# Hybrid decoder layer: seven block products instead of eight in both MLP matmuls, left factors kept in DRAM, MLP moved around the second attention

## The chip, the cores and the metric

The kernel runs on one core of a Trainium2 chip. The metric is the device time of one launch in microseconds. Inputs, weights and output are float32 in DRAM; one launch computes one decoder layer for 2048 tokens of width 1024.

## What is computed

The reference, cut to the parts that the change touches (the mixer, attention on dilated windows beside a gated linear recurrence, stays as it is):

```python
def reference(x, ...):
    h = rms_norm(x, mix_norm_pre)
    m = hybrid_mixer(h, w_in, ..., w_out)          # 2048 x 1024
    x = x + rms_norm(m, mix_norm_post)
    h = rms_norm(x, mlp_norm_pre)
    return x + rms_norm(squared_relu_mlp(h, w_ff_in, w_ff_out), mlp_norm_post)

def squared_relu_mlp(h, w1, w2):                   # w1 1024 x 4096, w2 4096 x 1024
    a = jax.nn.relu(h @ w1)
    return (a * a) @ w2
```

## The kernel before

Every large product is made of float32 operands that are split into a leading part and the rest (`split`, L51: a copy with rounding on ACT, L53, and a subtraction, L54, on DVE or GpSimd). A product of two split operands takes three matmuls on TensorE (leading by leading, leading by rest, rest by leading), each of one 128x128 block against 512 columns.

The work comes in these stages.

- **Input projection and first attention.** The 1024 x 2560 product `z` (L197 to L199) for all tokens, in two halves of 1024 tokens, the recurrent branch on four channel tiles (`recurrent_block`), and the attention of the first half of the queries, four pairs of heads (`attention`, hf 0). The string ORDER names the sequence of these pieces. q, k, v and the mixer's output `mix` go to DRAM (`scr`).
- **Output projection** of a half, eight tiles of 128 tokens (`out_proj_tile`, `proj_norm`): 48 matmuls of 128x512 into `m` (L615 to L617), then on ACT the sum of squares (L624), on DVE the norm (L66 to L74), the product with the gain (L626), the sum with x (L627), on ACT again a sum of squares; the result x2 goes to DRAM (L628). `make_h2` multiplies by the second norm (L593) and turns the tile with eight transposes on TensorE (L599), and splits it: h2, the MLP's input.
- **Second attention** (hf 1), four pairs of heads.
- **MLP** (`mlp`) in three passes: tokens 0 to 511, 512 to 1023, and 1024 to 2047. Each pass goes over the 32 blocks of the inner axis of 4096: `z = h2 @ w1` (L884 to L886, 24 matmuls for 512 tokens), relu and square on ACT (L888, L889), then `o = a @ w2` (L767 to L769), added up in SBUF on DVE (L773, `y`). In the second product the passes two and three take Strassen's seven products of half blocks instead of eight for eleven and fourteen of the sixteen pairs of inner blocks; the sums of blocks of `w2` (L726, GpSimd) and of `a` (L726, DVE) are made for each pair. The first product is plain in all passes. w1 and w2 are loaded and split once for each pass.

What sets the order: a scheduler at build time orders each engine's instructions by a simulated timeline, within the dependencies and the buffers of the pools. So the first pass of the MLP runs amid the second attention, the second output projection (OPT, H2T: at which pair of inner blocks a tile is put in) amid the second pass, and the third pass by itself. SP issues nearly all loads and stores in one queue, in order; GpSimd issues the stores of `mix` and x2 and, at the end of the first two passes (`finish_all`), four accumulating loads of x2 into `y` (L813) and four stores of the result (L814), each store behind the landing of its load.

```python
for t in range(NT):
    tt = tt0 + t
    v.scalar_tensor_tensor(out=y[t], in0=y[t], scalar=r[:, t:t + 1], in1=g4t[0], ...)   # L812
    g.dma_start(out=y[t], in_=scr["x2"][tt], accum_op=ALU.add)                          # L813
    g.dma_start(out=out[tt // NC, tt % NC], in_=y[t])                                   # L814
```

Names in the profile: `z` with h2Ha, h2Hb or h2La is the MLP's first product, `z` with hH the input projection; `o` the MLP's second product with `B`, `A` (seven products) or `w2t`, `a` (plain); `S`, `SB`, `pT`, `oA`, `oB` are the attention's scores, turned probabilities and values; `kh`, `kl`, `vb` its loads; `mraw`, `mH`, `mL` the output projection's input, raw and split.

Of the kernel before, what the change touches and what calls it, by code (L numbers as in the profile page):

```python
# [40 lines left out]
def by_residue(ap):  # L41
    """512 tokens as they are stored, by (residue mod 4, quotient)."""
    return ap.rearrange("p (c m) -> p c m", c=NC)


def in_time(ap):
    """512 tokens in the order of time, seen by (residue, quotient)."""
    return ap.rearrange("p (m c) -> p c m", c=NC)


def split(nc, hi, lo, src, lo_eng=None):  # L51
    """src = hi + lo exactly; hi carries the leading bits, lo the rest."""
    nc.scalar.copy(out=hi, in_=src)  # L53
    (lo_eng or nc.vector).tensor_tensor(out=lo, in0=src, in1=f32(hi), op=ALU.subtract)  # L54


def rsqrt_mean(nc, pool, ss, k, name, eps, e=None):
    """1 / sqrt(ss / D + EPS) for ss [P, k]."""
# [27 lines left out]
class Project:  # L86
    """Input projection and recurrent branch, one half of the tokens at a time."""
# [25 lines left out]
    def load_start(self, ct, px):  # L113
        """the first weights and the first block of x^T, as the first product needs them."""
# [16 lines left out]
    def load_norm(self, tb, px=None):  # L131
        """1 / rms of a block of tokens, tokens on partitions."""
# [17 lines left out]
    def load_x(self, tb, px=None, also=None):  # L150
        """x^T times the gain, split; the norm's factor comes in after the products."""
# [4 lines left out]
        for k in range(KT):  # L156
            # x waits in the place that the next part of the lower halves takes
# [21 lines left out]
    def spread_norm(self, tb):  # L179
        """The norm's factors of a block along the free axis, on all partitions."""  # L180
# [21 lines left out]
    def qkv(self, hf, pr):  # L202
        """q, k, v of a pair of heads."""
# [42 lines left out]
    def recurrent_consts(self, conv_w, conv_b, w_r, b_r, w_i, b_i, lam):  # L246
# [14 lines left out]
        # hs = softplus(-lam); log1p(e) = 2 atanh(e / (2 + e))  # L261
# [20 lines left out]
        # the last inputs of the convolution and the last state, per channel tile  # L282
# [5 lines left out]
    def recurrent(self, hf, cs, w=None, px=None, pz=None):  # L288
        """the recurrent branch of some channel tiles."""
# [5 lines left out]
    def recurrent_block(self, hf, c, b, wx, wg, px, pz):  # L295
# [20 lines left out]
        # sigmoid(z) = (1 + tanh(z / 2)) / 2  # L316
# [3 lines left out]
        # a = exp(-L); 1 - a^2 = tanh(L) (1 + a^2)  # L320
# [14 lines left out]
        # gelu(x) = x / 2 * (1 + tanh(sqrt(2 / pi) * (x + 0.044715 x^3)))  # L335
# [15 lines left out]
def attention(tc, p, ps, cst, scr, hf, mask_a_d, mask_b_d, bufs):  # L351
# [27 lines left out]
    def across(t, i):  # L379
        """the last run of a block of 512 tokens and the first of the next, seen as runs() does."""  # L380
        a = t[:, (i - 1) * TB + 3 * MR:(i + 1) * TB]
        return bass.AP(a.tensor, a.offset, [list(a.ap[0]), [3 * P + MR, 2], [P, NC], [1, MR]])

    def probs(part, n):
        tags, bufs, n = (("thA", "tlA"), 1, n) if part == "A" else (("thB", "tlB"), 2 - hf, n)
# [8 lines left out]
    def softmax_rows(st, u, cols, sp, sm, parts, mask, name):  # L394
        """exp(S + mask - max) of the parts (columns, width) of one bank, with max and sum."""
# [14 lines left out]
    def pair(pr):  # L410
        st = {k: p.tile([P, 2, 2, NQH], F32, tag=f"st{k}", bufs=2, name=f"st{k}{hf}_{pr}") for k in "AB"}
        na = p.tile([P, HT], F32, tag="na", bufs=1, name=f"na{hf}_{pr}")
        nb = p.tile([P, HT], F32, tag="nb", bufs=1, name=f"nb{hf}_{pr}")
        va = p.tile([P, NQH + hf, 2 * P], F32R, tag="va", bufs=1, name=f"va{hf}_{pr}")
        for c in range(NC):
            cs = slice(c * MR, (c + 1) * MR)
            if hf:
                t0 = TB + c * P + P - MR
                nc.sync.dma_start(out=f32(va[cs, 0, :]), in_=f32(scr["v"][0][pr][t0:t0 + MR, :]))
            for i in range(NBH):  # L420
                t0 = i * TB + c * P
                nc.sync.dma_start(out=f32(va[cs, hf + 4 * i:hf + 4 * i + 4, :]),
                                  in_=f32(scr["v"][hf][pr][t0:t0 + P, :].rearrange("(n m) d -> m n d", m=MR)))
        for u in range(2):
            h = 2 * pr + u
            n_ = f"{hf}_{h}"
            row = slice(u * HD, (u + 1) * HD)
            ud = slice(u * P, (u + 1) * P)
            qs = p.tile([P, HT], F32R, tag="qs", bufs=bufs, name=f"qs{n_}")
            kh = p.tile([P, NK], F32R, tag="kh", bufs=bufs, name=f"kh{n_}")  # L430
            kl = p.tile([P, NK], F32R, tag="kl", bufs=bufs, name=f"kl{n_}")
            vb = p.tile([P, NX * NC, P], F32R, tag="vb", bufs=1, name=f"vb{n_}")
# [727 lines left out]
```

## Time and profile before

| | |
|---|---|
| median of 3 launches | 2399.44 us (2397.65 to 2401.24) |
| span of the profiled execution, first to last instruction | 2394.6 us |
| median less that span | 4.84 us |
| TensorE, matmuls | 10798, busy 2287.9 us (96%) |
| VectorE (DVE) / ScalarE (ACT) / GpSimd (POOL) busy | 1637.8 / 1158.5 / 1047.8 us |
| moved by DMA | 298.96 MB, mean 125 GB/s |

How to read it: the span is one execution; the launch time has some microseconds around it. A busy share of TensorE counts overlapped matmuls once; an idle time is what no matmul covers. PEclk is the share of the full TensorE clock that was granted. Stages by time from the span's start: to about 640 us input projection and first attention, to 745 us the first output projection, to 1275 us the second attention with the first MLP pass, to 1750 us the second pass with the second output projection, then the third pass.

### The profile page before, as it was taken

Reading aid. Unit: us, or ns where it says so; the run is one execution under the profiler, and the core shown is the slowest. Engines: PE = TensorE matmul, PEld = TensorE weight load, DVE = VectorE, ACT = ScalarE, POOL = GpSimd, SP = SyncE. Lnnn points to the kernel's source line nnn. Section 1 sums busy time; section 2 is a strip of 40 time slices with the busy share of each in tenths; the row PEclk is TensorE's granted clock in tenths of the full one; section 3 lists DMA queues with packets and bytes.
Section 4 is the critical chain, followed back from the end, with each engine's and each line's share of the span. In section 5 each row is a group of like instructions: output and inputs, shape, how many; then the busy total and the mean of one; then the engine's idle time right before and its main releaser. Section 6 shows DMA issues by size and latency. Waiting matters only on the chain. (4 is left out here: it accounts for less than half of the span.)

```text
span 2394.6 us, 31821 instructions
## 1 busy us (share of the span) xinstructions
PE 2287.9 (96%) x10798; PEld 1873.9 (78%) x10798; DVE 1637.8 (68%) x2991; ACT 1158.5 (48%) x2353; POOL 1047.8 (44%) x820
## 2 busy tenths in 40 slices
PE   8989999999998999999999989999989999999997
PEld 6668878677886888888887768887778888888886
DVE  6848577983353566666775998669647777677676
ACT  7537465663234555555564544445363333333332
POOL 5543324446221113131323667555365555555544
PEclk9999999999999999999999999999999999999999
DMA  8364775217647464546465333344411111111114
GB/s 278 102 163 131 200 214 142 67 62 227 182 137 202 110 170 126 163 136 167 123 160 162 119 119 106 116 154 159 127 53 58 49 53 53 53 54 49 53 58 137
DMA packets 183058, 298.96 MB, mean 125 GB/s; under 512 B 20224, under 2 KB 79008, under 8 KB 182896
## 3 DMA queue, kind: packets, MB, share of 16 engines
q1 hardware_dynamic: 175376, 271.40, 38.7%
q0 software_dynamic: 7520, 25.53, 3.3%
q8 instruction: 86, 1.41, 0.2%
q14 instruction: 76, 0.62, 0.1%
HBM read 246.39 MB, written 50.46 MB: 124 GB/s over the span
## 5 line engine op out<-in xcount | busy, mean ns | idle before, releaser
L773 DVE TENSOR_TENSOR y<-o,y 128x512 f32<-128x512 f32 x464 | 307.4, 681 | 125.0 <-PE o L769 124.6
L54 POOL TENSOR_TENSOR w2t<-w2r,w2t 128x512 fp32r<-128x512 f32 x92 | 138.6, 1521 | 427.0 <-ACT w2t L53 423.0
L884 PE MATMUL z<-h2Ha,w1H 128*128 128x512 f32 x768 | 304.8, 397 | 9.5 <-ACT sq L888 9.2
L885 PE MATMUL z<-h2La,w1H 128*128 128x512 f32 x768 | 302.4, 394 | 0.0
L886 PE MATMUL z<-h2Ha,w1L 128*128 128x512 f32 x768 | 302.3, 394 | 0.0
L197 PE MATMUL z<-hH,wH 128*128 128x512 f32 x640 | 261.5, 409 | 15.9 <-ACT wH L53 7.4
L198 PE MATMUL z<-hL,wH 128*128 128x512 f32 x640 | 260.8, 408 | 0.6 <-DVE hL L172 0.6
L199 PE MATMUL z<-hH,wL 128*128 128x512 f32 x640 | 260.3, 407 | 0.0
L54 POOL TENSOR_TENSOR B<-w2r,B 128x512 fp32r<-128x512 f32 x125 | 195.0, 1565 | 86.8 <-ACT B L53 86.3
L767 PE MATMUL o<-B,A 128*128 128x512 f32 x546 | 211.7, 394 | 12.0 <-DVE y L773 7.0
L768 PE MATMUL o<-B,A 128*128 128x512 f32 x546 | 214.1, 392 | 1.6 <-POOL B L54 1.6
L53 ACT CAST w1H<-w1r 128x512 fp32r<-128x512 f32 x192 | 112.2, 619 | 212.7 <-PE z L885 169.2
L769 PE MATMUL o<-B,A 128*128 128x512 f32 x546 | 213.5, 392 | 1.5 <-DVE A L54 1.5
L884 PEld LDWEIGHTS z<-h2Ha,w1H 128*128 128x128 f32 x768 | 145.5, 190 | 41.3 <-ACT sq L888 11.3
L886 PEld LDWEIGHTS z<-h2Ha,w1L 128*128 128x128 f32 x768 | 145.7, 190 | 30.0
L885 PEld LDWEIGHTS z<-h2La,w1H 128*128 128x128 f32 x768 | 146.0, 190 | 29.5
L197 PEld LDWEIGHTS z<-hH,wH 128*128 128x128 f32 x640 | 122.5, 191 | 48.6 <-ACT wH L53 8.0
L768 PE MATMUL o<-w2t,a 128*128 128x512 f32 x400 | 157.7, 397 | 1.7 <-POOL w2t L54 1.7
L767 PE MATMUL o<-w2t,a 128*128 128x512 f32 x400 | 157.3, 402 | 0.1
L769 PE MATMUL o<-w2t,a 128*128 128x512 f32 x400 | 156.0, 394 | 0.0
L54 POOL TENSOR_TENSOR wL<-wraw,wH 128x512 fp32r<-128x512 f32 x74 | 103.9, 1418 | 111.4 <-ACT wH L53 92.8
L198 PEld LDWEIGHTS z<-hL,wH 128*128 128x128 f32 x640 | 122.3, 191 | 31.4 <-issue 4.3
(271 smaller groups left out, 5620.5 us busy)
## 6 DMA issues: line engine op xcount, KB each, us to landing
w1r<-in_dram SPq DMA_DIRECT2D x192, 256.0 KB, 2.8
w2r<-in_dram SPq DMA_DIRECT2D x192, 256.0 KB, 2.9
wraw<-in_dram SPq DMA_DIRECT2D x79, 256.0 KB, 3.6
kh<-sk SPq DMA_DIRECT2D x48, 256.0 KB, 5.9
kl<-sk SPq DMA_DIRECT2D x48, 256.0 KB, 7.6
vb<-sv SPq DMA_DIRECT2D x24, 512.0 KB, 5.0
xr<-in_dram SPq DMA_DIRECT2D x32, 256.0 KB, 5.8
xn<-in_dram SPq DMA_DIRECT2D x16, 512.0 KB, 6.8
```

What stands on the lines that cost most here:

```text
L53: nc.scalar.copy(out=hi, in_=src)
L54: (lo_eng or nc.vector).tensor_tensor(out=lo, in0=src, in1=f32(hi), op=ALU.subtract)
L197: pe.matmul(z, hi[:, k, :], hh, start=(k == 0), stop=False)
L198: pe.matmul(z, hi[:, k, :], hl, start=False, stop=False)
L199: pe.matmul(z, lo[:, k, :], hh, start=False, stop=(k == KT - 1))
L767: pe.matmul(o, a[:, 0, ts], b[:, 0, :], start=(j == 0), stop=False)
L768: pe.matmul(o, a[:, 0, ts], b[:, 1, :], start=False, stop=False)
L769: pe.matmul(o, a[:, 1, ts], b[:, 0, :], start=False, stop=(j == len(pairs) - 1))
L773: v.tensor_tensor(out=dst, in0=o, in1=dst, op=ALU.add)
L884: pe.matmul(z, wh[:, k, :], hh[:, k, :], start=(k == 0), stop=False)
L885: pe.matmul(z, wh[:, k, :], hl[:, k, :], start=False, stop=False)
L886: pe.matmul(z, wl[:, k, :], hh[:, k, :], start=False, stop=(k == KT - 1))
```

## The change

Both MLP products are made as Winograd's form of Strassen's scheme with seven products throughout, and the MLP goes by halves of 1024 tokens instead of three passes.

- **MLP input** (`mlp_in`): for two blocks of the inner axis at a time (a pair, 16 in a half), tokens and model axis in halves. Seven products of 12 matmuls of 128x512 (L844 to L846) go into three banks zA, zB, zC; sums of w1 blocks are made on GpSimd, the four results are put together on ACT and DVE in `sq`. Two pairs run interleaved (TURNS). The right factors are sums of blocks of h2 (`Factors`), made tile by tile in the output projection (`columns`) and at its end (`finish`). Of each pair the seven left factors of the second product (`a`, 1792 KB) are stored to DRAM; in the first half also the sums of w2 (1024 KB a pair, from a load of 1024 KB) for both halves. w1 is read once for each half (1024 KB a pair).
- **MLP output** (`mlp_out`): the seven products one after the other, each over all 16 pairs: a factor pair of 256 KB + 256 KB is loaded (L948 and L954 or L956), split on ACT, DVE and GpSimd, and used for 12 matmuls (L964 to L966), four banks of 128x512 accumulating over the 16 pairs in PSUM. The rings of split factors have 3 places in the first half and 16 in the second.
- **Place:** first output projection, MLP input of the first half, then the second attention with the steps of the first half's MLP output put between its own by a written order (`interleave`, two steps of three matmuls at each place, TensorE's order by hand), the load of w_out, the second output projection, then the second half's MLP input and output. The last piece of the input projection (q13) comes after the first attention's pools are closed.
- **Attention:** loads of the second half's keys as one DMA for both copies, buffers for the next head's loads, and its own pieces cut so that the next scores stand before the present values. Nothing of what it computes changes.

```diff
-def mlp(tc, p, pc, pw, ps, cst, scr, T, tt0, h2T, w1, w2, g4, out, nb1, nb2, ...):
...
+LEFT = {1: "A11", 2: "A12", 3: "S4", 4: "A22", 5: "S1", 6: "S2", 7: "S3"}
+RIGHT = {1: "B11", 2: "B21", 3: "B22", 4: "T4", 5: "T1", 6: "T2", 7: "T3"}
...
+class Factors:
+    EARLY, LATE = ("B11", "B21", "B22"), ("T2", "T3", "T1", "T4")
...
+    def columns(self, p, ps, ident, tt, x2, rs2, g3b):
+        v.scalar_tensor_tensor(out=h2, in0=x2, scalar=rs2[:, tt:tt + 1], in1=g3b, op0=ALU.mult, op1=ALU.mult)
+        for q in range(2):
...
+                nc.tensor.transpose(pt[:, i * P:(i + 1) * P], h2[:, k * P:(k + 1) * P], ident)
+            (v.tensor_copy if q else nc.scalar.copy)(out=R[q][th][:, :, cs], in_=pt.rearrange("p (k t) -> p k t", t=P))
+        if th == 0:
+            self.split("B11", b11, cs)
+            self.split("B21", b21, cs)
+        else:
+            e = v if c == TB // P - 1 else g
+            self.split("B22", b22, cs)
+            sums_right(lambda o, a, b, op: e.tensor_tensor(out=o[:, :, cs], ...), b11, b12, b21, b22)
...
+def mlp_in(tc, pm, px, ps, scr, hf, H, w1, w2):
...
+        def product(o, m, start):
+            hi, lo = f[m]
+            bh, bl = H[RIGHT[m]]
+            for k in range(KH):
+                pe.matmul(o, hi[:, k], bh[:, k], start=start and k == 0, stop=False, skip_group_check=True)
+                pe.matmul(o, hi[:, k], bl[:, k], start=False, stop=False, skip_group_check=True)
+                pe.matmul(o, lo[:, k], bh[:, k], start=False, stop=k == KH - 1, skip_group_check=True)
...
+        nc.sync.dma_start(out=scr["a"][hf][j][:, 0:3], in_=sq[:, 0:3])
+        nc.sync.dma_start(out=scr["a"][hf][j][:, 3:7], in_=A)
...
+TURNS = (0, 0, 1, 1, 0, 0, 1, 1, 0, 1, 0, 0, 1, 1)
...
+def mlp_out(tc, p, ps, ring, cst, scr, hf, w2, g4, out, px=None):
...
+    def factors(m, j):
+        al = p.tile([P, TB], F32R, tag="aL", bufs=ring, name=f"aL{n}")
+        cst["load"] = nc.sync.dma_start(out=f32(al), in_=scr["a"][hf][j][:, SCR[m]])
+        ah = p.tile([P, TB], F32R, tag="aH", bufs=ring, name=f"aH{n}")
+        split(nc, ah, al, f32(al))
+        br = p.tile([P, TB], F32, tag="bR", bufs=7 if hf else 4, name=f"bR{n}")
...
+        split(nc, bh, bl, br, lo_eng=g)
...
+    def finish(t):
+        sumsq(nc, p, ss, y[t], f"y{tt}")
+        if hf == 0:
+            r = rsqrt_mean(nc, p, ss, 1, f"y{tt}", cst["eps"])
+            v.scalar_tensor_tensor(out=y[t], in0=y[t], scalar=r, in1=g4b[0], op0=ALU.mult, op1=ALU.mult)
+            g.dma_start(out=y[t], in_=scr["x2"][tt], accum_op=ALU.add)
+            g.dma_start(out=out[tt // NC, tt % NC], in_=y[t])
+            return
...
+FIRSTFILL = 24
+ORDER2 = (1, 6, 5, 3, 2, 7, 4), (1, 2, 6, 7, 5, 4, 3)
...
+                with sb("at1", "right") as pa, pp("at1ps", "right") as paps, \
+                        tc.manual_schedule(engines={mybir.EngineType.PE}):
+                    interleave(attention(tc, pa, paps, cst, scr, 1, mask_a, mask_b, px), rest)
+                wo = load_wo(1, lambda: [next(rest, None) for _ in range(4)])
+                run_all(rest)
+            end = half(1, px, wo)
```

Counted in the built programs, the input projection's and the output projection's matmuls and the attention's are the same in number; the MLP's fall from 3072 + 2838 to 2688 + 2688, by 534.

TensorE at the end of the first output projection, before: after the last matmuls of tile 7 (`m7`) the first MLP product goes on (`z0_1`, block 1 of pass 0), whose input was turned tiles earlier.

```order
L615 MATMUL m7_6988<-woH0_3_6143,mH0_7_4_6982 128x512
L616 MATMUL m7_6988<-woL0_3_6144,mH0_7_4_6982 128x512
L617 MATMUL m7_6988<-woH0_3_6143,mL0_7_4_6983 128x512
L886 MATMUL z0_1_0_9741<-h2Ha0_6223,w1L0_1_9732 128x512
L884 MATMUL z0_1_0_9741<-h2Ha0_6223,w1H0_1_9731 128x512
L885 MATMUL z0_1_0_9741<-h2La0_6224,w1H0_1_9731 128x512
```

The same place now: the transposes of tiles 6 and 7 (`h2t6`, `h2t7`) stand between `m7` and the first matmul of the MLP input (`zA0`).

```order
L693 MATMUL m7_7078<-woH0_3_5920,mH0_7_4_7072 128x512
L694 MATMUL m7_7078<-woL0_3_5921,mH0_7_4_7072 128x512
L695 MATMUL m7_7078<-woH0_3_5920,mL0_7_4_7073 128x512
L789 MATMUL h2t6_0_7040<-ident_60,h2_6_7038 128x128 x4
L789 MATMUL h2t6_1_7046<-ident_60,h2_6_7038 128x128 x4
L789 MATMUL h2t7_0_7157<-ident_60,h2_7_7155 128x128 x4
L789 MATMUL h2t7_1_7163<-ident_60,h2_7_7155 128x128 x4
L844 MATMUL zA0_0_7249<-hHB11_0_6231,fH0_0_1_7255 128x512
L845 MATMUL zA0_0_7249<-hLB11_0_6232,fH0_0_1_7255 128x512
```

What moved: in the queue of TensorE nothing stands any more between the last tile's product and its own transposes. The end of the second half's output projection reads the same.

GpSimd where the first 512 tokens are finished, before: the accumulating loads (`y0_`) and stores (`out_0_dram`) stand in the midst of the second pass, ahead of a join of the attention and the next split of w2 (`w2t4`); the first `mL` of the second output projection stands 68 rows behind.

```order
L813 DMA y0_0_9680<-sx20_119 128x1024
L813 DMA y0_1_9681<-sx21_120 128x1024
L813 DMA y0_2_9682<-sx22_121 128x1024
L814 DMA out_0_dram<-y0_0_9680 128x1024
L813 DMA y0_3_9683<-sx23_122 128x1024
L814 DMA out_0_dram<-y0_1_9681 128x1024
L814 DMA out_0_dram<-y0_2_9682 128x1024
L814 DMA out_0_dram<-y0_3_9683 128x1024
L563 TENSOR_TENSOR na1_3_9024<-na1_3_9024,co1_3_0_0_9649 128x512
L564 TENSOR_TENSOR nb1_3_9025<-nb1_3_9025,co1_3_0_1_9650 128x512
L54 TENSOR_TENSOR w2t4_1_1_12747<-w2r4_0_1_1_12745,w2t4_1_1_12747 128x512
```

GpSimd now, at the end of the first half's MLP output: the tokens 512 to 1023 (`y0_4` to `y0_7`) and behind them the first split of the second output projection (`mL1_0`, tile 0).

```order
L991 DMA y0_4_10393<-sx24_123 128x1024
L647 DMA smix1_3_114<-na1_3_12923 128x512
L991 DMA y0_5_10394<-sx25_124 128x1024
L991 DMA y0_6_10395<-sx26_125 128x1024
L992 DMA out_0_dram<-y0_4_10393 128x1024
L991 DMA y0_7_10396<-sx27_126 128x1024
L992 DMA out_0_dram<-y0_5_10394 128x1024
L992 DMA out_0_dram<-y0_6_10395 128x1024
L992 DMA out_0_dram<-y0_7_10396 128x1024
L54 TENSOR_TENSOR mL1_0_0_15116<-mraw1_0_0_15110,mH1_0_0_15115 128x512
L54 TENSOR_TENSOR mL1_0_4_15125<-mraw1_0_4_15119,mH1_0_4_15124 128x512
```

What moved: the split that TensorE's next product (the third matmul of `m` for tile 0) needs stands right behind the last store. The first four tiles (`y0_0` to `y0_3`) are finished amid the second attention, between splits of the right factors (`bL`).

More of the change, by code (lines that the diff above doesn't have):

```diff
@@ L348, in scr_cols, with attention @@
     return t[:, b * TB:(b + 1) * TB]
[L351 removed]
+def attention(tc, p, ps, cst, scr, hf, mask_a_d, mask_b_d, px=None):
     nc = tc.nc
@@ new lines, in interleave, with fill @@
+def interleave(units, rest):
+    def fill(n):
+        for _ in range(n):
+            next(rest, None)
+    todo, loads = [], []
+    for pr in range(NP):
+        parts, ending, load = units(pr)
+        todo += [[*x, None] for x in parts]
+        todo[-1][-1] = ending
+        loads += load
+    n = len(todo) // len(loads)
+    for _ in range(4):
+        fill(FIRSTFILL // 4)
+        loads[0](False)
+    loads.pop(0)
+    for f in todo[0][0]:
+        f()
+        fill(2)
+    for k, (_, turn, values, ending) in enumerate(todo):
+        ahead = todo[k + 1][0] if k + 1 < len(todo) else [lambda: None] * 2
+        if k % n < 4 and loads:
+            loads[0](False)
+            if k % n == 3:
+                loads.pop(0)
+        turn[0]()
+        fill(2)
+        ahead[0]()
+        fill(2)
+        turn[1]()
+        fill(2)
+        ahead[1]()
+        fill(2)
+        values()
+        if ending:
+            fill(2)
+            ending()
@@ L1089, in trunk @@
[L1089 to L1094 removed]
+            with sb("at0", "right") as pa, pp("at0ps", "right") as paps:
+                attend = attention(tc, pa, paps, cst, scr, 0, mask_a, mask_b)
+                run(ORDER)
+            wo = load_wo(0)
+            run(LATER)
```

874 lines of the change are left out of this document (453 added, 421 removed).

## The prediction, written before the changed kernel was run

> **What bounds the kernel now.** I read the busy times of the page first.
>
> ```profile
> PE 2287.9 (96%) x10798; PEld 1873.9 (78%) x10798; DVE 1637.8 (68%) x2991; ACT 1158.5 (48%) x2353; POOL 1047.8 (44%) x820
> ```
>
> TensorE is busy for 96% of the span, no other engine for over 68%; the chain of waits names only the last microseconds, so it says nothing here. Next the windows view, by stage (stretch, length, busy time of PE, PEld, DVE, ACT, POOL, granted clock, DMA share, GB/s).
>
> ```profile
> 0.00:640.00 640.00, 599.19 (x2916) 478.92 (x2917) 427.82 (x889) 349.37 (x714) 277.44 (x257) 0.98 0.55 161
> 640.00:745.00 105.00, 103.74 (x475) 85.76 (x474) 53.76 (x109) 44.17 (x90) 27.23 (x25) 1.00 0.46 146
> 745.00:1275.00 530.00, 505.25 (x2682) 426.59 (x2682) 337.04 (x814) 297.96 (x686) 118.97 (x96) 0.98 0.55 152
> 1275.00:1750.00 475.00, 450.02 (x1971) 364.82 (x1969) 370.82 (x555) 221.85 (x435) 273.18 (x200) 0.98 0.41 128
> 1750.00:2340.00 590.00, 587.83 (x2576) 483.48 (x2577) 411.43 (x562) 231.49 (x402) 326.36 (x223) 1.00 0.18 53
> 2340.00:2395.00 55.00, 41.86 (x185) 34.31 (x183) 36.97 (x66) 13.65 (x29) 24.61 (x21) 0.93 0.45 149
> ```
>
> Length less PE gives TensorE's idle time: 40.8, 1.3, 24.75, 24.98, 2.2 and 13.1 us. Both ends stay; the two middle stages, 49.7 us, are rebuilt by the change. So the time is a count of matmuls at a pace, and some stalls. The pace, from the groups and from PE's timeline (start, length):
>
> ```profile
> L768 PE MATMUL o<-B,A 128*128 128x512 f32 x546 | 214.1, 392 | 1.6 <-POOL B L54 1.6
> ```
> ```profile
> 1900.04 0.39 PE L769 MATMUL o<-B,A 128*128 128x512 f32 x1
> ...
> 1901.40 0.39 PE L769 MATMUL o<-B,A 128*128 128x512 f32 x1
> ```
>
> A matmul's row is 0.39 us long, but matmuls overlap: six starts in 1.36 us, **0.2267 us** each. That, and not 392 ns, is what one less saves. The sum is made against the span of 2394.6 us; the median of the runs, 2399.44, is 4.84 above it.
>
> **Matmuls.** 534 fewer, at 0.2267: **−121.1**. The sums that pay for it lie on the other engines. For a pair of the MLP input (84 matmuls, 19.0 us) these rows price them:
>
> ```profile
> L53 ACT CAST w1H<-w1r 128x512 fp32r<-128x512 f32 x192 | 112.2, 619 | 212.7 <-PE z L885 169.2 <-DMA w1r<-in_dram 43.2
> L54 DVE TENSOR_TENSOR w1L<-w1r,w1H 128x512 fp32r<-128x512 f32 x132 | 102.9, 799 | 45.0 <-ACT w1H L53 43.7 <-DMA w1r<-in_dram 1.0
> L54 POOL TENSOR_TENSOR B<-w2r,B 128x512 fp32r<-128x512 f32 x125 | 195.0, 1565 | 86.8 <-ACT B L53 86.3
> ```
>
> ACT some 18 operations (seven splits, three copies, eight of relu and square) at 0.62 = 11.2; DVE seven splits and seven adds at 0.80 = 11.2; GpSimd four sums of w1 and four of w2 at 1.57 = 12.5. All lie beside 19.0; without that cover the largest overhang would count 32 times. Output: GpSimd one split, 1.57, per group of 12 matmuls (2.72). Nothing for these.
>
> **The old middle.** Its order is gone, so its idle goes: **−49.7**. The half clock after stalls goes too:
>
> ```profile
> 1408.98 0.49 PE L767 MATMUL o<-B,A 128*128 128x512 f32 x1
> 1414.39 0.79 PE L884 MATMUL z<-h2Ha,w1H 128*128 128x512 f32 x1 [4.91 <-ACT sq L888]
> 1414.98 0.63 PE L885 MATMUL z<-h2La,w1H 128*128 128x512 f32 x1
> 1415.40 0.63 PE L886 MATMUL z<-h2Ha,w1L 128*128 128x512 f32 x1
> ```
> ```profile
> 1408.00:1418.00 10.00, 5.09 (x16) 3.68 (x15) 9.37 (x12) 4.47 (x9) 6.33 (x6) 0.83 0.34 105
> ```
>
> After 4.91 idle the starts are 0.42 apart, and the ten microseconds ran at 0.83: 1.7 lost beside the idle time. Clock 0.98 over 1005 us is 20 lost, which go; some seven long stalls, below, bring back 12: **−8**.
>
> **Output projection to MLP input, two times.** TensorE waits now for the last tile's norm chain. The same chain for an earlier tile:
>
> ```profile
> 646.60 1.02 ACT L624 ACTIVATE x<-m 128x1024 f32<-128x1024 f32 x1
> ...
> 648.79 1.28 DVE L626 SCALAR_TENSOR_TENSOR x<-m,r_m,g2b 128x1024 f32<-128x1024 f32 x1
> ...
> 651.68 1.22 DVE L627 TENSOR_TENSOR x<-x,xt 128x1024 f32<-128x1024 f32 x1
> ...
> 652.93 1.06 ACT L632 ACTIVATE xt<-x 128x1024 f32<-128x1024 f32 x1 [1.25 <-DVE x L627]
> ...
> 658.74 2.33 DVE L593 SCALAR_TENSOR_TENSOR h<-x,rs,g3b 128x1024 f32<-128x1024 f32 x1
> ...
> 661.12 1.09 PE L599 MATMUL h2t<-ident,h 128*128 128x128 f32 x8 [1.26 <-DVE ms_m L66]
> ```
>
> It took 14.5 us; some 4 of it, between 653.9 and 658.7, are other work on DVE, so 10.5 at least. I take 11.5 each, near the lower end since nothing else is left to do: **+23** (21 to 29).
>
> **The finish on GpSimd.** A waiting instruction holds up what stands behind it: the accumulating loads wait for `y`, each store for its load, and behind the fourth store stands `mL1_0`, for which TensorE's next product waits. The same sequence before:
>
> ```profile
> 1237.49 0.68 DVE L773 TENSOR_TENSOR y<-o,y 128x512 f32<-128x512 f32 x1
> ```
> ```profile
> 1244.86 0.95 POOL L813 DMA_DIRECT2D y<-sx  x1 [5.49 <-DVE y L812]
> ...
> 1261.09 0.53 POOL L814 DMA_DIRECT2D out_dram<-y  x1 [4.82 <-DMA y<-sx]
> ```
>
> GpSimd took 16.8 us from 1244.86 to 1261.62, and the whole from the last `y` 24.1. Ahead of it come 4.2 us on ACT and DVE (a copy out of the bank 0.62, a sum of squares 1.06, scalars 1.2 as between the ends of 647.62 and 648.79 above, one multiplication 1.28), behind it 1.3 for `mL`, a bit under the 1.57 of a split: **+22.3** (up to 25.4, that is 24.1 and 1.3). Hidden before, since TensorE had MLP work. For the first four tiles it stands amid the attention, ahead of `bL` splits; the ring holds some three groups and the attention's steps lie between: **+5** (0 to 10).
>
> **Second attention.** Among the groups of 745 to 1275 there are six of MLP matmuls, the first 266, the last 258, together 1572:
>
> ```profile
> L884 PE MATMUL z<-h2Ha,w1H 128*128 128x512 f32 x266 | 106.2, 400 | 2.8 <-ACT sq L888 2.8
> ...
> L767 PE MATMUL o<-w2t,a 128*128 128x512 f32 x258 | 103.8, 407 | 0.0
> ```
>
> They took 356 us, so the attention itself about 146. Now 1344 stand beside it, 305 us, in a written order: a little less cover, better spread, so I keep the idle time per busy time, 24.75 in 505, on some 450: **+22** (11 to 45, half to twice that share). What may come late is the ring of three (rivals). Fifty-two of the products stand together ahead of it: 13 groups whose own chain, landing 2.9, ACT 0.62, DVE 0.80, is 4.3 against a lead of two groups of 2.72: **+4** (0 to 13).
>
> **MLP input's slots and small edges.** The sums of w2, `sq` and the left factors share four buffers, and each waits for a store to land; on SP the loads of w1 stand behind such a load. **+4** (0 to 40). Out_proj's tiles without MLP work between them: **+3** (0 to 19, a chain of 14.5 against 48 matmuls of 10.9 and a look-ahead). MLP input to MLP output, whose first factors are the last to be stored: **+4** (0 to 8.6). Tail, before:
>
> ```profile
> 2381.47 0.39 PE L769 MATMUL o<-w2t,a 128*128 128x512 f32 x1
> ...
> 2389.69 1.42 DVE L860 SCALAR_TENSOR_TENSOR yg<-yg,st,x2e 128x512 f32<-128x512 f32 x2
> ```
>
> From there 13.1 us to the end, three adds of the last banks among them; now the last bank is read directly by the sum of squares and the gain: 8 left, **−5**.
>
> Sum: −121.1 −49.7 −8 +23 +22.3 +5 +22 +4 +4 +3 +4 −5 = **−96.5**: span 2298.1, **time 2303**.
>
> **The rivals.**
>
> *Dense order.* TensorE's hand-written order and deep buffers leave few of the new stalls. For it: 1750 to 2340 has 2.2 us idle in 590. Half of the +87 stays away: about **2259**. Chance 0.20.
>
> *A transfer bounds a stage.* The MLP input of the first half moves per pair 1024 (w1) + 1024 (w2) + 1792 (left factors) + 1024 KB (sums of w2) = 4.98 MB in 19.0 us, 261 GB/s. Two stretches of before:
>
> ```profile
> 0.00:60.00 60.00, 52.14 (x211) 39.52 (x212) 39.91 (x85) 44.96 (x75) 30.52 (x46) 1.00 0.82 278
> 300.00:360.00 60.00, 55.34 (x323) 46.78 (x323) 43.91 (x129) 38.38 (x103) 16.19 (x13) 0.97 0.79 214
> ```
>
> At a DMA share near 0.8 they moved 278 and 214. At 278 a pair fits; at 214 it takes 23.3, 4.2 more, 16 times +68: **2371**. Chance 0.18. I take the higher rate as likelier, since three fifths of it are whole blocks of weights and their sums, as the loads of the first stretch are; the left factors are the rest.
>
> *The ring of three decides: slower.* Of 448 us with 112 groups, one group takes about 4.0. A slot is free again after landing + 0.62 + 0.80 + its group's 4.0, over three slots: it binds once a landing takes over 6.5 us.
>
> ```profile
> w2r<-in_dram SPq DMA_DIRECT2D x192, 256.0 KB, 2.9
> ...
> kl<-sk SPq DMA_DIRECT2D x48, 256.0 KB, 7.6
> ```
> ```profile
> DMA to landing us min/median/max: 5.5/7.5/9.5
> ```
>
> The factors are 256 KB in one piece like `w2r` (2.9), but stand in SP's queue among the attention's loads (7.6). At 7.6 it costs (7.6 − 6.5)/3 × 112 = 41: 2343. At the longest landing shown, of the accumulating loads, 9.5: +111, **2414**; slower than before from 9.2 on. Against it: DMA's share in that stage was 0.55. Chance 0.08. The Trainium skill ("DMA: Bandwidth & Descriptors", section "Latency and other measured facts") puts memory latency at 0.2 us on average and 2 us at high load; by it a 2.9 us landing would grow by 1.8 to an estimated 4.7, the ring would never bind, and the sum would stay at 2303. The row of 7.6 speaks against so small a growth.
>
> *The change doesn't do what it says*, so that no matmuls are saved on the path: 0.02, within 0.2%; the counts of the built program speak against it.
>
> **How the numbers follow.** Forecast 0.52, dense 0.20, transfer 0.18, ring 0.08, nothing 0.02. The range runs from the dense case, 2255, to the transfer case, 2375; the ring case, and a tenth beside these ends, are left out. A measurement here tells 0.2% (4.8 us) from no change. Faster 0.90, same 0.02, slower 0.08.
>
> **What would show it.** 10264 matmuls; after the last `m7` in both halves an idle time of 10.5 to 14.5 us ended by `h2`'s product; ahead of `mL1_0` one of 20 to 25 with GpSimd in L991 and L992; in the second attention about 5% idle, ended by `bL` or `kl`; the MLP input's pair near 19 us in both halves. Were the first half's pair at 23 and the second's at 19, transfers bound it; were the waits in the attention on `aL` with landings over 6.5, the ring. It is wrong if the MLP input or output stages by themselves show idle time of over 5%, or the time lies outside the range.

## The result, and the profile after

The changed kernel takes 2790.1 us (2782.2 to 2794.4, four runs) against 2398.6 of the kernel before: 1.163 times as long, 95% interval 1.160 to 1.166. The forecast was 2303, within 2255 to 2375, faster with a chance of 0.90. The profiled execution has a span of 2790.5 us, 492 more than the 2298.1 that the sum came to.

The busy line of the page first. The forecast had 2158.8 us of busy TensorE (2287.9 less 121.1 less 8) and 139.3 of idle time; here are 2269.0 and 521.5. So 382 of the 492 us are waits and 110 are matmuls that took longer.

```profile
PE 2269.0 (81%) x10264; PEld 1826.7 (65%) x10264; DVE 1391.2 (50%) x2502; ACT 1240.1 (44%) x2437; POOL 1039.7 (37%) x851
```

The windows view by stage, columns as before. The stages are: input projection and first attention; first output projection; MLP input of the first half; second attention with the first half's MLP output; second output projection; the second half's MLP input; its MLP output.

```profile
0.00:730.00 730.00, 609.56 (x2894) 486.42 (x2895) 415.94 (x889) 349.30 (x713) 273.31 (x255) 0.92 0.44 136
730.00:859.00 129.00, 100.62 (x451) 81.15 (x450) 72.89 (x120) 45.45 (x90) 55.84 (x44) 0.88 0.42 137
859.00:1181.00 322.00, 315.93 (x1347) 253.70 (x1345) 205.35 (x238) 170.39 (x302) 185.16 (x132) 0.99 0.64 235
1181.00:1945.00 764.00, 489.35 (x2373) 402.27 (x2374) 277.50 (x670) 291.67 (x640) 188.38 (x165) 0.81 0.45 135
1945.00:2116.00 171.00, 113.85 (x517) 92.01 (x517) 99.75 (x173) 63.08 (x126) 73.24 (x63) 0.84 0.50 162
2116.00:2432.00 316.00, 314.87 (x1345) 253.18 (x1345) 172.89 (x234) 171.34 (x299) 84.98 (x60) 1.00 0.35 128
2432.00:2791.00 359.00, 324.81 (x1347) 257.96 (x1345) 146.89 (x180) 148.84 (x270) 178.82 (x132) 0.93 0.59 197
```

Both MLP inputs are as dense as thought (6 and 1 us idle). The second attention takes 764 us where 451 of work were counted, 275 of them idle, at a DMA share of 0.45: neither TensorE nor the transfers as a whole are full. And the first stage, which the forecast left alone, takes 730 us instead of 640, with 120 idle. What do they share? The waits of TensorE (line, what ended the wait: us in total, times, longest):

```profile
PE oA L529 <- ACT thA L53: 106.4, 9, 17.4
PE o L964 <- ACT aH L53: 99.5, 16, 29.0
PE h2t L789 <- DVE h L782: 43.2, 2, 21.6
PE m L693 <- ACT mH L53: 42.1, 2, 35.4
```

One wait of 12.2 us in the second attention, followed back. ACT's timeline: the cast of the probabilities, `thA`, stands in ACT's order behind the cast `aH`, and that one waited for the landing of `aL`, 15.4 us.

```profile
1361.94 0.62 ACT L53 CAST aH<-aL 128x512 fp32r<-128x512 f32 x1 [15.44 <-DMA aL<-sa]
...
1362.98 0.58 ACT L53 CAST thA<-pT 128x512 fp32r<-128x512 f32 x1
```
```profile
1363.61 0.58 PE L529 MATMUL oA<-thA,va 128*128 128x256 f32 x1 [12.21 <-ACT thA L53]
```

SP's queue around it: `aL` was issued at 1349.59, so its 256 KB landed about 12 us later. Ahead of it in the queue stand the two loads of `kh`; behind it the two of `kl`, whose issuing took SP 8.9 us.

```profile
1336.59 1.05 SPq L432 DMA_DIRECT2D kh<-sk  x2
...
1349.59 1.15 SPq L948 DMA_DIRECT2D aL<-sa  x1
1350.79 8.92 SPq L432 DMA_DIRECT2D kl<-sk  x2
```

And the windows of that time, four microseconds each:

```profile
1352.00:1356.00 4.00, 0.00 (x0) 0.00 (x0) 0.00 (x0) 0.00 (x0) 0.00 (x0) 0.72 0.24 87
1356.00:1360.00 4.00, 0.00 (x0) 0.00 (x0) 0.00 (x0) 0.00 (x0) 0.00 (x0) 0.50 0.13 53
1360.00:1364.00 4.00, 0.39 (x1) 0.29 (x1) 1.41 (x2) 1.62 (x3) 0.84 (x1) 0.50 0.13 52
```

In the first two of these windows all five engines stand still, and the DMA engines do nearly so: from 1356 on a share of 0.13 and 52 to 53 GB/s, where a stretch of before held 278. A share of 0.13 is as much as two engines of sixteen (0.125); the traces give the mean of the sixteen, not single engines. The load in flight is the change's "one DMA for both copies" of the keys: 512 KB, made by an access pattern whose outermost dimension is the two copies, with stride zero. At 52 GB/s that is an estimated 10.1 us a load, 20 for two. That `aL` came late because parts of it queue on those same two engines is argued from this, not shown. The Trainium skill ("DMA: Bandwidth & Descriptors", section "Rules for kernel authors") states this case: an outermost dimension of c under 16, a zero-stride broadcast of c copies for one, confines the whole DMA to at most c engines. The trace agrees, with a share of 0.13 for c of 2. The prediction did not weigh it.

### The profile page after: what moved, and what is told of

Same layout as the page of the kernel before. It is cut to its first block, busy times and chain, and to the rows that moved or that the text cites. A ratio compares the mean times of both kernels' runs of the same rounds, so it can differ in the third digit from the quotient of the medians.

```text
span 2790.5 us, 31033 instructions
## 1 busy us (share of the span) xinstructions
PE 2269.0 (81%) x10264; PEld 1826.7 (65%) x10264; DVE 1391.2 (50%) x2502; ACT 1240.1 (44%) x2437; POOL 1039.7 (37%) x851
## 4 chain that ended last, share of the span: by engine, by line
PE 42%; DMA 19%; issue 13%; DVE 9%; POOL 8%; ACT 3%; SPq 3%; POOLq 0%; DVEq 0%; ACTq 0%
DMA aL<-sa 8%; POOL bL L54 6%; PE zA L844 4%; PE zA L846 4%; PE zA L845 4%; PE m L695 2%; PE m L694 2%; PE m L693 2%; PE zC L846 2%; PE zC L845 2%; PE zC L844 2%; DMA wraw<-in_dram 2%; PE o L966 2%; PE o L964 2%; PE o L965 2%
## 5 line engine op out<-in xcount | busy, mean ns | idle before, releaser
L54 POOL TENSOR_TENSOR bL<-bR,bH 128x512 fp32r<-128x512 f32 x224 | 305.5, 1371 | 685.8 <-ACT bH L53 682.9
L54 DVE TENSOR_TENSOR aL<-aL,aH 128x512 fp32r<-128x512 f32 x224 | 198.0, 893 | 555.3 <-ACT aH L53 549.8
L964 PE MATMUL o<-bH,aH 128*128 128x512 f32 x896 | 373.8, 424 | 111.3 <-ACT aH L53 99.5
L965 PE MATMUL o<-bL,aH 128*128 128x512 f32 x896 | 366.8, 409 | 3.5 <-POOL bL L54 3.5
L966 PE MATMUL o<-bH,aL 128*128 128x512 f32 x896 | 363.6, 409 | 6.2 <-DVE aL L54 6.0
L53 ACT CAST aH<-aL 128x512 fp32r<-128x512 f32 x224 | 138.7, 619 | 478.2 <-DMA aL<-sa 475.7
L964 PEld LDWEIGHTS o<-bH,aH 128*128 128x128 f32 x896 | 178.6, 200 | 150.7 <-ACT aH L53 106.9
L54 DVE TENSOR_TENSOR fL<-w1r,fH 128x512 fp32r<-128x512 f32 x160 | 153.2, 961 | 164.4 <-ACT fH L53 164.0
L966 PEld LDWEIGHTS o<-bH,aL 128*128 128x128 f32 x896 | 176.8, 197 | 52.6 <-DVE aL L54 14.0
L965 PEld LDWEIGHTS o<-bL,aH 128*128 128x128 f32 x896 | 178.8, 200 | 39.0 <-POOL bL L54 7.9
L529 PE MATMUL oA<-thA,va 128*128 128x128 f32 (+1 forms) x152 | 45.6, 321 | 136.9 <-ACT thA L53 106.4
```

The source lines that it names most:

```text
L964: pe.matmul(o, ah[:, ts], bh, start=fresh and j == 0, stop=False, skip_group_check=True)
L965: pe.matmul(o, ah[:, ts], bl, start=False, stop=False, skip_group_check=True)
L966: pe.matmul(o, al[:, ts], bh, start=False, stop=j == NJ - 1, skip_group_check=True)
```

## The experiments

**Theory A**: the key loads for both copies run on two DMA engines, and what stands behind them on SP's queue waits some 10 us a load. **Theory B**: it is the ring of three that the prediction named as its slower rival, whatever the form of the loads. The first four runs tell them apart.

**Keys by 64 partitions, in both attentions.**

```diff
-nc.sync.dma_start(out=f32(t[:, x * HT:(x + 1) * HT]), in_=f32(twice(scr["k"][x][pr][u, a])))
+for i in range(2):
+    nc.sync.dma_start(out=f32(t[i * HD:(i + 1) * HD, x * HT:(x + 1) * HT]), in_=f32(scr["k"][x][pr][u, a]))
```

> The changed kernel with one edit: each load of keys for both copies (512 KB, one DMA whose outer dimension is the two copies) is made as two DMAs of 64 partitions, as before. Theory A (such a load runs on two of the sixteen DMA engines; while it does, 52 GB/s and a DMA share of 0.13 to 0.24, the factors behind it on SP's queue wait some 10 us): second attention from 764 us to 480 to 520, first stage from 730 to about 650, time 2790 to about 2430 (2380 to 2500). Theory B (the ring of three is too short beside the attention's loads, whatever their form): the bytes and the queue are the same, so the time stays within 2% of 2790.

Measured: 2462.9 us, 1.026 (1.023 to 1.029) of before. 327 us are gone, by making the same bytes as two DMAs of 64 partitions each. The busy line, and the windows of the first stage and of the second attention:

```profile
PE 2226.1 (91%) x10264; PEld 1793.2 (73%) x10264; DVE 1397.4 (57%) x2502; ACT 1237.4 (50%) x2435; POOL 1043.3 (42%) x851
```
```profile
0.00:640.00 640.00, 597.61 (x2896) 477.18 (x2896) 428.65 (x889) 347.76 (x712) 276.11 (x255) 0.98 0.53 155
...
1085.00:1628.00 543.00, 475.20 (x2438) 392.33 (x2439) 280.26 (x686) 297.78 (x651) 200.47 (x177) 0.94 0.71 195
```

The first stage is as before; the second attention is 543 us instead of 764, its idle time 68 instead of 275. It stays above the 480 to 520 expected; the time is within the 2380 to 2500, above its middle of 2430. Theory B's "within 2% of 2790" is out.

**The same in the second attention alone** (with the old line kept for `hf == 0`).

> As the first, in the second attention alone; the first attention keeps the loads for both copies. Theory A: the first stage stays at 730 us, the rest is as in the first run: 70 to 90 us more than that, about 2510. Theory B: within 2% of 2790.

Measured: 2560.2 us, 1.067 (1.064 to 1.070), 97 more than with both, where 70 to 90 were expected. The first stage is as in the changed kernel, with 121 us idle:

```profile
0.00:730.00 730.00, 608.80 (x2892) 486.83 (x2892) 416.47 (x887) 349.43 (x713) 274.35 (x255) 0.92 0.45 135
```

So of the 327 us, 97 came from the first attention, where no MLP and no ring stand beside it, and 230 from the second.

**A ring of four instead of three, key loads as changed.**

```diff
-rest = mlp_out(tc, p, ps, 3, cst, scr, 0, w2, g4, out)
+rest = mlp_out(tc, p, ps, 4, cst, scr, 0, w2, g4, out)
-br = p.tile([P, TB], F32, tag="bR", bufs=7 if hf else 4, ...)
+br = p.tile([P, TB], F32, tag="bR", bufs=7 if hf else 3, ...)
-SMB = (3, 4)
+SMB = (3, 3)
```

> The changed kernel, key loads as they are, with four places instead of three in the ring of split factors of the first half's MLP output (one buffer less for the raw right factors and one less for the scores, for space). Theory A: each of some 18 stalls of 9 to 18 us in the second attention is shorter by one group, up to 4 us: 2720 (2700 to 2780). Theory B: a landing may be 10.5 instead of 6.5 us before the ring binds, so most of the stage's 275 us idle goes: below 2600.

Measured: 2810.9 us, 1.171 (1.168 to 1.174): no gain at all, rather a loss of 0.7%. B's "below 2600" is missed by far, and so are A's 70 us. The edit also takes a place each from the raw right factors (`bR`) and from the scores, so it doesn't show what a longer ring alone would do. The waits only changed their place; the longest line is now a turn of probabilities that waits for a buffer's split:

```profile
PE pT L376 <- DVE tlA L54: 162.7, 11, 19.7
PE oA L529 <- ACT thA L53: 44.6, 3, 17.9
```

**The kernel before with the key loads for both copies.**

```diff
-for i in range(2):
-    nc.sync.dma_start(out=f32(t[i * HD:(i + 1) * HD, x * HT:(x + 1) * HT]), in_=f32(scr["k"][x][pr][u, a]))
+k = scr["k"][x][pr][u, a]
+k = bass.AP(k.tensor, k.offset, [[0, 2], *[list(z) for z in k.ap]])
+nc.sync.dma_start(out=f32(t[:, x * HT:(x + 1) * HT]), in_=f32(k))
```

> The kernel before with the key loads of the changed kernel alone (one DMA for both copies). Theory A: 24 times two loads take 10 us each instead of about 2 on the queue that all loads share; the first attention loses what the changed kernel's lost, some 80 us, the second some 50 to 150: about 2550 (2450 to 2650). Theory B: without the ring it costs nothing: within 1% of 2399.

Measured: 2757.6 us, 1.149 (1.146 to 1.151). This one edit makes the kernel before 355 us slower, more than the 50 to 250 expected, with no ring and no other part of the change. TensorE waits for the keys themselves:

```profile
PE S L470 <- DMA kl<-sk: 151.6, 9, 20.3
PE S L470 <- DMA kh<-sk: 113.7, 9, 17.4
```

The longest, 20.3 us, is as long as two loads of the estimated 10.1. So the form of the key loads is the cause, in either kernel. Is it that the same bytes are read more than once, and not the outermost dimension of two? The kernel before has loads that read one row 128 times, with 128 outermost (`partition_broadcast`), also of 512 KB:

```profile
g4b<-in_dram SPq DMA_DIRECT2D x3, 512.0 KB, 3.9
```

They land in 3.9 us (median), and one that was alone in flight, issued at 2324.01, moved 344 GB/s at a DMA share of 0.89 in its first full microsecond. Repetition as such is not slow there. What follows asks what the other 160 us are, between the mended kernel (2462.9) and the forecast.

**Ring of four on the mended kernel** (the edits of the third run on the first).

> Keys by 64 partitions as in the first run (2462.9), and four places instead of three in the first half's ring (one buffer less for raw right factors, one less for scores). If the ring of three is what leaves 68 us of TensorE idle in that run's second attention: 40 us or more less, below 2425. If with the loads on all engines the factors come early enough and the idle time is the attention's own chains and the burst of loads at its start: 0 to 20 less, 2445 to 2465.

Measured: 2456.0 us, 1.022 (1.020 to 1.025), 7 less, and the intervals of the two runs overlap. The idle time of the stage is 70 us over the same stretch, so this ring with one raw buffer less gains nothing there. The waits moved: those of the whole run on `aH` fell from 35.5 to 15.4 us, those on `bH`, whose raw buffers are one fewer, rose from 12.4 to 27.7. A longer ring with all its raw buffers was not tried.

**Left loads first, in the second half's MLP output.** The windows of the changed kernel show 34 us idle in its last stage, where the forecast had the tail of 8 and a small edge. On SP the order there is a right factor some seven groups ahead, then a left one:

```profile
2711.00 0.33 SPq L954 DMA_DIRECT2D bR<-in_dram  x1
2711.43 0.37 SPq L948 DMA_DIRECT2D aL<-sa  x1
```
```profile
2709.16 0.80 PE L964 MATMUL o<-bH,aH 128*128 128x512 f32 x1 [1.96 <-ACT aH L53]
```

```diff
+with tc.issue_after(cst["load"].ins) if hf else contextlib.nullcontext():   # behind the left factor's load
     nc.sync.dma_start(out=br, in_=...)                                      # right factor
```

> Keys by 64, and in the second half's MLP output each load of a right factor stands behind the load of its left factor on SP. Theory D (SP, ACT and GpSimd wait for each other in a circle: a right load waits for GpSimd's split, that one for ACT behind the cast of a left factor, whose load stands behind a right load; so groups come every 2.95 us instead of 2.72, and the last product, which wants all sixteen in 11 us, waits): the 33 us of idle time and some 10 of half clock at its end go: about 2420 (2410 to 2435). Rival (the 193 GB/s that the stage asks for are too much): no change, 2455 to 2470.

Measured: 2429.2 us, 1.011 (1.009 to 1.014), 34 less, by order alone, as expected of theory D. The last stage before (first run) and now:

```profile
2101.00:2457.00 356.00, 322.94 (x1346) 256.95 (x1344) 146.82 (x180) 148.75 (x270) 178.64 (x132) 0.93 0.60 199
```
```profile
2106.00:2427.00 321.00, 308.43 (x1348) 254.31 (x1346) 144.17 (x181) 155.70 (x270) 177.94 (x132) 0.99 0.67 221
```

Some 20 us of the gain are idle time (33 to 13), the rest matmuls that no longer run at the lower clock (0.93 to 0.99). It moves 221 GB/s now, so the rate was not the limit; the loading order was, by the circle of SP, ACT and GpSimd that the expectation describes. This kernel is the base of the later runs but the next two.

**No accumulating loads** (on the first run's kernel).

```diff
-g.dma_start(out=y[t], in_=scr["x2"][tt], accum_op=ALU.add)
```

> Keys by 64, without the eight accumulating loads of the first half's finish: its output lacks the sum with x2. The prediction's mechanism (GpSimd's sequence of loads and stores sets the start of the second output projection): 17 to 22 us less, about 2443. Theory E (the 4 MB of w_out and the mixer's output behind them on SP end last, GpSimd was done 6 us earlier): within 6 us of 2463.

Measured: 2458.5 us, 1.023 (1.020 to 1.025), 4 less, which the intervals do not tell from none. The wait ahead of the second output projection falls from 34.8 to 27.7 us. The prediction's mechanism, worth 17 to 22 us, is out: without the loads GpSimd's last store is out at 1647.9, the first cast of the mixer's output comes at 1660.8, and most of the wait stays.

**The norm ahead of the splits** (on the first run's kernel).

```diff
-split(nc, hi, lo, src)
+with tc.issue_after(last.ins) if j < 2 else contextlib.nullcontext():    # last: the last tile's h2
+    split(nc, hi, lo, src)
```

> Keys by 64, and the splits of the first two pairs' left factors of the MLP input stand behind the last tile's norm on VectorE, in both halves. Theory F (the chain from the last tile's product to its transposes is 21.8 us of idle time and not 11.5 because these splits stand before it, two of them at 3.6 us beside GpSimd's sums): 6 to 9 us less for each half and some half clock, about 2445 (2438 to 2452). Rival (the chain alone takes that long): within 4 us of 2463.

Measured: 2462.5 us, 1.026 (1.023 to 1.028): no change. The wait that it was made for did shrink, from 43.2 us for the two halves to

```profile
PE h2t L790 <- DVE h L783: 28.9, 2, 14.4
```

but the splits still have to be made, and those of the right factors that follow come later: TensorE waits 4.2 us for one on VectorE at 775, and 6.1 us for one on ACT at 1801. So 10.3 of the 14.3 us came back in another place. That the work at this edge is the bound, and not its order, is argued from that.

**Every second right load left out** in the first half's MLP output.

```diff
+if hf == 0 and j % 2:
+    br = keep[m, j - 1]          # no load
```

> On the sixth run's kernel (keys by 64, left loads first; 2429.2): every second load of a right factor in the first half's MLP output is left out, the one before is used again (its output is another). 56 of 112 loads of 256 KB go, 14.7 of some 106 MB that the stage moves. Theory H (in the second attention what is left, some 68 us of idle time, is the transfers' rate: DMA share 0.71, up to 1.0 at its start): 25 us or more less, below 2404. Rival (the attention's own chains over ACT and VectorE): 0 to 12 less, 2417 to 2430.

Measured: 2419.1 us, 1.008 (1.007 to 1.009), 10 less. The stage's rate falls from 195 GB/s, its idle time only from 72 us (sixth run, same stretch) to 68:

```profile
1085.00:1628.00 543.00, 474.70 (x2440) 394.04 (x2440) 279.33 (x691) 299.01 (x654) 197.95 (x173) 0.93 0.63 168
```

So there the transfers' rate is not the bound; the rival holds as to its size. That the rest are the attention's own chains is argued from that, not shown.

**w_out's raw tiles elsewhere.**

```diff
-with sb(f"wr{hf}", "right") as pr:
+with sb(f"wr{hf}", "left" if hf else "right") as pr:
```

> On the sixth run's kernel: the raw tiles of the second w_out lie in other memory than the output projection's tiles, so that the loads of the mixer's output need not wait for their splits; the order on SP is the same. Theory E (what TensorE waits for in the 36 us is the 4 MB of w_out and behind them the mixer's output on SP's queue): the mixer's loads come some 5 to 10 us earlier, TensorE's wait goes from 36 to about 28: 2419 to 2426. Rival (GpSimd's finish with its stores): no change.

Measured: 2432.1 us, 1.013 (1.012 to 1.015): no change, and TensorE's wait went from 36.1 to 39.7 us, where theory E had 28. SP's and ACT's timelines of this run:

```profile
1633.20 17.45 SPq L676 DMA_DIRECT2D wor<-in_dram  x8
...
1667.00 0.33 SPq L1232 DMA_DIRECT2D g3b<-in_dram  x1
1667.42 2.75 SPq L725 DMA_DIRECT2D mraw<-smix  x6
```
```profile
1657.45 1.14 ACT L53 CAST woH<-wor 128x512 fp32r<-128x512 f32 x2 [11.77 <-DMA wor<-in_dram]
...
1665.03 1.14 ACT L53 CAST woH<-wor 128x512 fp32r<-128x512 f32 x2 [1.09 <-DMA wor<-in_dram]
```

The edit did not free the mixer's loads. The load of a norm's gain, `g3b`, stands ahead of them on SP, and now it waits 15.5 us for the raw tiles' last landing and split; the mixer's loads (`mraw`) start at 1667.4, where in the sixth run they were issued between 1650.7 and 1665.1. So this run tells nothing against theory E's second half. It does show how late the weights are: the 4 MB of w_out arrive over 32 us. Of the 17.45 us that SP takes to issue them, 13.4 are waits for the mixer's last store on GpSimd, and from 1641 to 1666 the DMA share is 0.99 to 1.05, with the finish's 4 MB of loads and stores beside them. The seventh run puts the accumulating loads at 7 us of the wait; how the rest is shared between the weights and the mixer's output stays open.

**Twelve steps ahead of the attention instead of 24.**

```diff
-FIRSTFILL = 24
+FIRSTFILL = 12
```

> On the sixth run's kernel (2429.2): 12 instead of 24 steps of the MLP output ahead of the second attention. Three groups (12 steps) are in the ring, and the fourth group's factors stand behind the attention's first loads: TensorE waits 16 us for them at 1102. Theory I (with 12 steps it goes on to the attention's scores as soon as their keys are in, and 12 steps, 8.2 us, are left to cover the wait for w_out at 1631): 10 to 20 us less, 2409 to 2419. Rival (the keys come no sooner, and the steps taken from the start cover nothing): within 5 us of 2429.

Measured: 2429.2 us, 1.012 (1.010 to 1.014): no change, as the rival has it, though not by its mechanism. The wait for w_out did fall, from 36.1 to 29.6 us. But at the start one wait of 15.6 us for `aH` became three of 21.1 together, PE's timeline shows:

```profile
1111.91 0.55 PE L506 MATMUL S<-kh,qa 128*128 128x256 f32 x1 [9.62 <-DMA kh<-sk]
1117.13 0.55 PE L506 MATMUL S<-kl,qa 128*128 128x256 f32 x1 [4.67 <-DMA kl<-sk]
1124.91 0.79 PE L966 MATMUL o<-bH,aH 128*128 128x512 f32 x1 [6.80 <-ACT aH L53]
```

**TensorE kept busy in three long waits.**

```diff
+for i in range(n):               # n = 180, 280, 180
+    tc.keep_in_program_order(nc.tensor.transpose(pt[:, ...], ident, ident))    # read by nobody
```

> On the sixth run's kernel: TensorE makes transposes that nobody reads in the three long waits (180 ahead of the last tile's in both output projections, where it waits 21.8 us; 280 ahead of the second output projection, where it waits 36). Theory G (after a long wait TensorE runs at half clock for some microseconds more, 3 to 5 us for each, not the 1.7 of the prediction): 8 to 14 us less, 2415 to 2421. Rival (1.7 us each): 5 less, 2424. If the transposes end after what was waited for, slower.

Measured: 2425.0 us, 1.010 (1.008 to 1.011), 4 less, with intervals that overlap. The granted clock of the two stages went from 0.90 and 0.83 (tenth run, same windows) to

```profile
640.00:767.00 127.00, 118.64 (x623) 98.96 (x620) 72.79 (x120) 43.86 (x88) 55.07 (x44) 0.96 0.44 139
...
1628.00:1790.00 162.00, 154.00 (x928) 133.38 (x927) 93.98 (x161) 59.67 (x118) 70.32 (x60) 0.98 0.52 164
```

and it was worth some 4 us for three waits. That is the rival's 5 rather than theory G's 8 to 14, but the difference is too near the noise to give a size for one wait. The sixth run's trace does: after the wait of 21.6 us TensorE starts at 765.8 and the windows read a clock of 0.50 to 769 and 1.00 from 770; after the 36.1 us it starts at 1667.7 and they read 0.50 to 1674 and 1.00 from 1675. Half of these 4 and 7 us is an estimated 2 and 3.5 lost. Much of a low granted clock in a stage lies in the idle time itself, where it costs nothing.

**All together** (the edits of the first, fifth, sixth, eleventh and twelfth run).

> All together: keys by 64, left loads first, ring of four (one buffer less for raw right factors and for scores), 12 steps ahead of the attention, TensorE busy in the three long waits. Sum of the single differences (7 for the ring, 4 for the busy waits, 10 to 20 for the fill, from 2429.2): 2398 to 2408, about the time before; if the waits only change places: 2412 to 2425.

Measured: 2419.5 us, 1.008 (1.006 to 1.010), within the 2412 to 2425 of the waits that only change places. No kernel tried here is faster than the one before.

## Why the prediction was wrong, point by point

**The step that failed** is one that is not in the sum. The front part lists "loads of the second half's keys as one DMA for both copies" among the edits (the code has it in both attentions), and the prediction gave it no price: "Now 1344 stand beside it ... so I keep the idle time per busy time" took the loads as they were; its one row of a key load is the old `kl`, 7.6 us for 256 KB. A load of the new shape takes an estimated 10.1 us for 512 KB, at 52 GB/s, and what stands behind it waits. Undoing it gives back 327 of the 487 us between forecast and result. "Both ends stay" failed for the same reason: the first attention loads its keys the same way, 97 us.

**The slower rival** had the right sign and the right sight, left factors that come late from a queue shared with the attention, at a chance of 0.08; its mechanism was another. Landings did go past its 6.5 and 9.2 us (12 us for the `aL` above), but with the mended loads the time fell by 327 us beside the same ring of three, and a fourth place, with one raw buffer less, brought nothing with either form of the loads. Its 2414 fell short in part since a late factor also held up ACT, where the attention's casts stand behind it (106.4 us of waits on `thA`). By the Trainium skill's latency at high load ("DMA: Bandwidth & Descriptors", section "Latency and other measured facts") the landing was an estimated 4.7 us, and the ring would have held. The same row of 12 us speaks against using it here, since what was late was a queue.

**Matmuls**, −121.1: the count is right (10264). The pace is right in the MLP output, but in the MLP input six starts take 1.40 us, 0.2333 each:

```profile
1000.05 0.40 PE L845 MATMUL zA<-hLT,fH 128*128 128x512 f32 x1
...
1001.45 0.40 PE L845 MATMUL zA<-hLT,fH 128*128 128x512 f32 x1
```

For 2688 of them that is 18 us less gained. It is so in the second half too, at 128 GB/s, so the transfers don't explain it; the cause stays open.

**Half clock**, −8: the 1.7 for a long wait is near the 2 estimated after 21.6 us of idle time, and half of the 3.5 after 36.1 us (twelfth run). The mended kernel with left loads first still has 2209.3 us of busy TensorE, 50 over the forecast, 18 of them the pace above; the others are not taken apart.

**Output projection to MLP input**, 11.5 each: 21.6. The chain alone is 14.4 (eighth run), the upper end of its row; the first left factors' splits, put on VectorE ahead of it, are 7.2, and moving them mostly moved the wait. "Nothing else is left to do" was the false step: the next stage's work is on the same engine.

**The finish on GpSimd**, +22.3: a wait of 35.4 us is at that place, but it was not the last to end. GpSimd's last store, the two loads on SP and the cast that released TensorE, in the changed kernel:

```profile
1987.06 0.53 POOL L992 DMA_DIRECT2D out_dram<-y  x1 [5.45 <-DMA y<-sx]
```
```profile
1959.57 16.73 SPq L675 DMA_DIRECT2D wor<-in_dram  x8
...
1977.49 14.32 SPq L724 DMA_DIRECT2D mraw<-smix  x8
```
```profile
1993.97 1.33 ACT L53 CAST mH<-mraw 128x512 fp32r<-128x512 f32 x2 [6.30 <-DMA mraw<-smix]
```

GpSimd is free at 1987.6; the mixer's output, behind w_out on SP, is there at 1994.0. The prediction followed the order of one queue and didn't ask what the other queue had to bring in at the same time. Of the sequence 7 us count (34.8 to 27.7 in the seventh run), as load on the transfers.

**The second attention** beside this: 68 us idle in the mended kernel against 22 and 5, and 4 (0 to 13) at its start, where one wait is 15.8. A half of the right loads less and another place in the ring gave 10 and 7 us of time, but hardly any of this idle time; what it is stays open.

**MLP input to output**, +4 (0 to 8.6): 6.2 and 5.6 us of waiting, 11.8 together, above its range.

**Not in the sum**: the last stage's circle of three engines, 34 us; and 6.6 us ahead of the first output projection, where TensorE waits for the mixer's output; before, the longest wait of that stage was 1.3.

**Slips in the sums**: 505 less 356 is 149 us of attention, not 146, and at 7.6 us the ring's time is 2344, not 2343. Neither moves the forecast.

**Right**: the MLP input's slots (6 and 1 us idle for 4), the MLP input bounded by no transfer (235 GB/s, a pair about 20 us), the output projections' tiles (nothing idle beside the waits at their two ends, for 3), and the tail: the last matmul starts at 2782.66, 7.8 us ahead of the end, for 8.

## What to carry to other kernels

Read every edited DMA by the outermost dimension of its pattern, also where the bytes and the count of DMAs get better: a broadcast of two copies in one DMA moved 52 GB/s where one of 128 copies moved 344, and its price was paid by what stood behind it. A DMA share of 0.13, near 2/16, while all engines wait was its sign in the windows view. And a loading order in which one engine's load stands behind another's free buffer should be followed once around the circle, since neither deep rings nor the mean rate show it.

## What the runs showed of the hardware

A DMA whose outermost dimension is two moved 52 to 53 GB/s at a share of 0.13, an estimated ten microseconds for 512 KB, where one of the same size with 128 outermost landed in 3.9 (median). A 256 KB load issued behind such loads landed 12 us later. Issuing itself then took 8.9 us for two DMAs on SP, against 1.05 for the two before. MLP input matmuls of 128x512 start 0.2333 us apart where those of the MLP output, of the same shape, start 0.2267 apart, at a granted clock of 0.99 to 1.00. After 21.6 and 36.1 us without matmuls the clock read 0.50 for some 4 and 7 us of work.
